# Six turns instead of three in a projection unit, and other addresses for the low halves, in a two-layer attention trunk on one core

## The chip, the core and the metric

One NeuronCore of a Trainium2 chip runs the whole program in one launch. The metric is device time in microseconds (us); lower is better. Three runs of the kernel before gave 625.53, 626.4 and 626.1, a median of 626.1 us.

## What is computed

A trunk of two layers over 256 tokens of 1024 channels, in float32. Each layer normalises its input, multiplies it by one wide matrix of 9808 columns, and cuts the result into the operands of three token mixers (a causal one, one that keeps 64 keys chosen by an indexer, and one with forget gates), their SiLU gates, and three sets of merge gates:

```python
h = rms_norm(x, gain)
proj = jnp.einsum('bsd,de->bse', h, w_in)
...
y = jnp.einsum('nbsw,nwd->bsnd', jnp.stack([oa, ob, oc], axis=0), w_branch)
gates = jax.nn.sigmoid(merge_logit).reshape(B, S, N_BRANCH, D_MODEL)
merged = jnp.sum(gates * y, axis=2)
return x + jnp.einsum('bsd,de->bse', merged, w_out)
```

A final RMS norm follows the second layer.

## The kernel before

Every large product is made of three products of rounded parts. An operand is split into a high half (the value rounded to the matmul's float32r type) and a low half (the rest), and high times high, high times low and low times high are summed in PSUM. So a weight tile `raw` becomes `wh` (ScalarE, line 364) and `wl` (VectorE, line 368), 128x1024 each, in rings of six buffers. The normalised, transposed input of a layer lies in `hTh` and `hTl`; gated mixer outputs lie in `og0h`, `og0l`, `og1h`, `og1l`; the merged result of a layer is put into the two buffers `V` that held the mixers' values.

TensorE's work comes in units, each of which fills one PSUM bank. `unit_b` (line 419) makes 128 projected columns for all 256 tokens: 16 matmuls with `wh` as stationary operand, going through `hTh` and `hTl` of each of eight blocks in turn, and 8 matmuls with `wl`, which meet `hTh` alone. All 24 move 256 columns and all load weights of their own. There are 130 such units. `unit_y` (line 867) multiplies gated outputs by the branch matrices: 12 matmuls of 256 columns, in 48 units. `unit_a` (line 435) has the weights as the moving operand, mostly 512 columns, and `hTh`/`hTl` (mixer values) or the merged halves (output projection) as the stationary one.

The order in a unit is a list `g`, cut into four operations for the planner (line 429):

```python
g = his[:8] + los[:2] + his[8:11] + los[2:5] + his[11:] + los[5:]
for a, b in ((0, 8), (8, 13), (13, 21), (21, 24)):
```

A step from a `wh` matmul to a `wl` matmul is called a turn here; a unit has three, after 8, 11 and 16 of the `wh` matmuls. The second comes behind a matmul that moves `hTh`, the others behind one that moves `hTl`.

Nothing of the order is left to the hardware's queues: `Plan.run` (line 137) goes through all operations with estimated durations and puts them on the engines, for each engine the ready operation of the lowest key among those that could start soonest. A unit's key is its number; the splits of its weights have that number less `SPLIT_LEAD` (line 41), and attention steps (scores, transposes of the probabilities on line 678, products with the values on lines 695 to 700) have keys of their own. Such steps go between a unit's four operations, never inside one. I call a stretch of such steps inside or between units a block.

A tile's address in SBUF follows from the order in which tiles are made. Bytes modulo 512 of the tiles that matter: `wh` 128, `wl` 0, `hTh` and `hTl` both 192, both `V` buffers 128, the `og` tiles 192.

Of the kernel before, what the change touches and what calls it, by code (L numbers as in the profile page):

```python
# [9 lines left out]
F32 = mybir.dt.float32  # L10
F32R = mybir.dt.float32r
# [4 lines left out]
S = 256  # L16
# [3 lines left out]
KC = D // 128  # L20
# [17 lines left out]
       ("DVE", "DVE"): 127.0, ("ACT", "ACT"): 127.0, ("POOL", "POOL"): 100.0, ("ACT", "SP"): 1500.0, ("DVE", "SP"): 1500.0}  # L38
SEM = 70.0
HALF = 95.0  # L40
SPLIT_LEAD = 2.0
MARGIN = 200.0
QK_MARGIN = 1000.0
WARM = 14
MTH = 8
NC1 = 4
DMA_KEY = (-95, -94, -85, -84)
HI_KEY = (-60, -48, -47, -46)
NB1 = 2
EARLY = 1.5  # L50
HT_KEY = (-50, -49.5, -46.8, -46.2)
BANKS = ("proj", "s", "t", "o")
# [176 lines left out]
def t_mm(n):  # L229
    return 1.3 + 0.4434 * n  # L230
# [3 lines left out]
def hybrid_trunk(ctx, tc, x, norm_gain, w_in, forget_bias, w_branch, w_out, final_gain, consts, out):  # L234
# [3 lines left out]
    pool = ctx.enter_context(tc.tile_pool(name="sb", bufs=1))  # L238
# [3 lines left out]
    plan = Plan()  # L242

    def tag(name, n, shape, dt=F32):
        plan.tag(name, [pool.tile(shape, dt, name=f"{name}{i}") for i in range(n)])
# [4 lines left out]
    def T(b):  # L250
        return b.slot[1]
# [7 lines left out]
    def act(fn, n, ps, reads, writes, key, name="", extra=0.0, touch=()):  # L259
        return plan.op([("ACT", t_act(n, ps) + extra, fn)], reads, writes, key, 0.0, name, touch)  # L260

    def dve(fn, n, reads, writes, key, name="", cost=None, touch=(), port=False):
        o = plan.op([("DVE", cost or t_dve(n), fn)], reads, writes, key, 0.0, name, touch)
        o.port = port
        return o
# [6 lines left out]

    wh = [pool.tile([128, 1024], F32R, name=f"wh{i}") for i in range(R_RING)]
    fz = pool.tile([128, 6, 16], F32, name="fz")
    wl = [pool.tile([128, 1024], F32R, name=f"wl{i}") for i in range(R_RING)]
    fbias = pool.tile([128, L, 8], F32, name="fbias")
    csum = pool.tile([128, 2, 8], F32, name="csum")
    V = [pool.tile([128, 2, 8, 128], F32R, name=f"v{i}") for i in range(2)]  # L280
    qs = [[pool.tile([128, S], F32R, name=f"q{p}{i}") for i in range(3)] for p in "hxy"]
    gT = pool.tile([128, L, KC], F32, name="gT")
    hTh = pool.tile([128, KC, S], F32R, name="hTh")
    hTl = pool.tile([128, KC, S], F32R, name="hTl")
    og = [[pool.tile([128, 4, S], F32R, name=f"og{i}{p}") for p in "hl"] for i in range(2)]
    NBD = 3
    bd = [[pool.tile([128, 2, S], F32R, name=f"bd{i}{p}") for p in "hl"] for i in range(NBD)]
# [15 lines left out]
    isc = pool.tile([128, 384], F32, name="isc")  # L303
    selb = pool.tile([128, 384], F32, name="selb")
    wf = pool.tile([128, S], F32, name="wf")
    cT = wf[:, :]
    half = pool.tile([128, 1], F32, name="half")
    small = pool.tile([128, 2, 4], F32, name="small")
    fsum = pool.tile([128, 2, 5], F32, name="fsum")
    ncs = pool.tile([128, 2, 8], F32, name="ncs")  # L310
    widx = pool.tile([128, 2, 8], F32, name="widx")

    k_id, k_rope, k_gT, k_bdz, k_cst, k_fb, k_wf, k_widx, k_lf, k_cs, k_main = (Tok() for _ in range(11))
    k_cT, k_row = Tok(), [Tok() for _ in range(6)]
# [7 lines left out]
    k_V = [[[Tok() for _ in range(2)] for _ in range(4)] for _ in range(2)]  # L322
    k_og = [[[Tok() for _ in range(4)] for _ in range(2)] for _ in range(2)]
    k_acc = [Tok() for _ in range(KC)]

    tag("raw", R_RAW, [128, 2048])
    plan.tag("wh", wh)
    plan.tag("wl", wl)
# [4 lines left out]
    plan.tag("ptl", pts[1:])  # L333
    plan.tag("bd", bd)
    for nm, n, cols, dt in (("rsh", 2, S, F32), ("rr", 2, S, F32),
                            ("th", 2, S, F32), ("g", 4, S, F32), ("e", 4, 384, F32), ("st", 8, 8, F32),
                            ("fb", 2, 384, F32), ("ot", 2, S, F32), ("t8", 4, 8, F32), ("mth", MTH, S, F32)):
        tag(nm, n, [128, cols], dt)
    ptag("proj", 3)
    ptag("s", 2)  # L340
# [6 lines left out]
    def piece(key, ckey, ap, cshape, sel, shape, k):  # L347
# [18 lines left out]
        def lo():  # L366
            p[1].v = T(p[1])[:, :a * b].rearrange("p (a b) -> p a b", a=a)
            DVE.tensor_tensor(p[1].v, sel(c.v), p[0].v.bitcast(F32), op=ALU.subtract)  # L368
        act(hi, a * b, False, [c], [p[0]], k - SPLIT_LEAD, f"hi {key}")
        dve(lo, a * b, [c, p[0]], [p[1]], k - SPLIT_LEAD, f"lo {key}", port=True)  # L370
        return p
# [31 lines left out]
    def mm_ops(o, terms, cost, writes, key, name, first, last, main=False):  # L403

        n = len(terms)

        def emit():
            for i, (a, b, _) in enumerate(terms):
                PE.matmul(o(), a(), b(), start=first and i == 0, stop=last and i == n - 1)  # L409
        reads = list({id(r): r for t in terms for r in t[2]}.values())  # L410
        pe(emit, cost * n, reads, writes + ([k_main] if main else []), key, name)
# [3 lines left out]
    def unit(name):  # L415
        units[0] += 1
        return units[0] - 1
# [3 lines left out]
    def unit_b(name, get, npart=128):  # L421
        u = unit(name)
        p = get(u)
        ps = Buf("proj")
        o = lambda: T(ps)[:npart, :S]
        his = [(lambda k=k: p[0].v[:, k], lambda k=k, h=h: h[:, k], [p[0]] + hT_all[i])
               for k in range(KC) for i, h in enumerate((hTh, hTl))]
        los = [(lambda k=k: p[1].v[:, k], lambda k=k: hTh[:, k], [p[1]] + hT_all[0]) for k in range(KC)]
        g = his[:8] + los[:2] + his[8:11] + los[2:5] + his[11:] + los[5:]
        for a, b in ((0, 8), (8, 13), (13, 21), (21, 24)):  # L430
            mm_ops(o, g[a:b], t_mm(256), [ps], u, name, a == 0, b == 24, True)
        return u, ps

# [16 lines left out]
    def rope(ps, key, np_=128):  # L450
        c, s = rope_t
        sh, r = Buf("rsh"), Buf("rr")
        a = lambda: T(ps)[:np_, :S]
        dve(lambda: DVE.stream_shuffle(T(sh)[:np_], a(), SWAP), S, [ps], [sh], key, "rope")  # L454
        gps(lambda: POOL.tensor_tensor(T(sh)[:np_], T(sh)[:np_], s[:np_], op=ALU.mult), S, [k_rope], [sh], key, "rope")  # L455
        dve(lambda: DVE.tensor_tensor(T(r)[:np_], a(), c[:np_], op=ALU.mult), S, [ps, k_rope], [r], key, "rope")  # L456
        gps(lambda: POOL.tensor_tensor(T(r)[:np_], T(r)[:np_], T(sh)[:np_], op=ALU.add), S, [sh], [r], key, "rope")  # L457
        return r

    def new_bd():  # L460
        b = Buf("bd")
        return b, [[Tok(), Tok(), Tok()] for _ in range(2)]
# [133 lines left out]
    class Pair:  # L596
# [3 lines left out]
        def ev_q(self, ps, key):  # L600
            key -= EARLY
            if self.mixer == "c":
                self.q = write_q((lambda: T(ps)[:, :S], ps), True, key, -0.125)
            else:
                r = rope(ps, key)
                self.q = write_q((lambda: T(r), r), False, key, -0.125)

        def ev_k(self, ps, key):
            self.k, self.kt = new_bd()
            src = ps if self.mixer == "c" else rope(ps, key - EARLY)  # L610
            write_bd(src, self.k, self.kt, key - EARLY, self.mixer == "c")
            self.attend(key + 1)

        def ev_g(self, ps, key):
            th = Buf("th")
            g = self.g = Buf("g")
            key -= EARLY
            act(lambda: ACT.activation(T(th), T(ps)[:, :S], AF.Tanh, scale=0.5), S, True, [ps], [th], key, "g")
# [22 lines left out]
        def attend(self, key):  # L641
# [43 lines left out]
            o = Buf("o")  # L685
            v = V[self.vi]

# [163 lines left out]
    def unit_m(l, n, j, gates):  # L851
        c0 = COL["mg"] + n * D + (j // 2) * 256
        u, ps = unit_b(f"m{n}{j}", lambda k: win_b(l, c0, j % 2, k))
        if n == 0:
            act(lambda: ACT.activation(acc[:, j], T(ps)[:, :S], AF.Tanh, scale=0.5), S, True, [ps], [k_acc[j]], u - EARLY, "mth")
            return
        th = gates[n, j] = Buf("mth")
        act(lambda: ACT.activation(T(th), T(ps)[:, :S], AF.Tanh, scale=0.5), S, True, [ps], [th], u - EARLY, "mth")

    def merged(j):  # L860
        v = V[j // 4].rearrange("p t h c -> p (t h c)")
        i = j % 4
        return [v[:, (2 * i + p) * S:(2 * i + p + 1) * S] for p in range(2)]

    k_mg = [k_V[j // 4][j % 4] for j in range(KC)]

    def unit_y(l, n, j, oi, gates, rank):
        u = unit(f"y{n}{j}")
# [73 lines left out]
    def v_units(l, m, vi):  # L942
        gets = [lambda k, i=i: rows_a("A", w_in, l, COL["v" + m], i, k) for i in range(4)]
        for t in range(2):
            ra = [lambda k, p=p, t=t: [k_hT[p][t][k]] for p in range(2)]
            u, ps = unit_a(f"v{m}{t}", gets, t, hA[0], hA[1], ra)
            v_out(ps, t, vi, [ps], u)

    def v_out(ps, t, vi, deps, key):
        hi, lo = V[vi][:, t, :, :64], V[vi][:, t, :, 64:]  # L950
        src = lambda: T(ps).rearrange("p (h c) -> p h c", h=8)
        kv = [k for i in (2 * t, 2 * t + 1) for k in k_V[vi][i]]
        act(lambda: ACT.activation(hi, src(), AF.Copy), W, True, deps, kv, key, "v", touch=[ps])
        dve(lambda: DVE.tensor_tensor(lo, src(), hi.bitcast(F32), op=ALU.subtract), W, deps, kv, key, "v", touch=[ps])
# [69 lines left out]
    def alternate(a, b):  # L1024
        r = []
        for i in range(0, max(len(a), len(b)), 2):
            r += a[i:i + 2] + b[i:i + 2]
        return r
# [4 lines left out]
    for l in range(L):  # L1033
# [21 lines left out]
        v_units(l, "b", 0)  # L1055
        for f in between(mixer(l, "b", 0, 0), alternate(y_of(l, 2, 1, 1, gates, range(8)), m_of(l, 1, gates, range(NB1)))):
            f()
        for f in m_of(l, 1, gates, range(NB1, 8)) + y_of(l, 1, 0, 2, gates, range(8)):
            f()
# [49 lines left out]
```

## Time and profile before

| | |
|---|---|
| median of three runs | 626.1 us (625.53 to 626.4) |
| the profiled execution | 625.54 us, span 623.6 us |
| PE busy | 612.1 us, 98% of the span, 4808 matmuls |
| DVE busy | 541.2 us, 87% |
| ACT busy | 450.6 us, 72% |
| POOL busy | 89.1 us, 14% |
| read from HBM | 103.37 MB |
| granted TensorE clock | 0.999 of full speed |

The profiled execution is 0.56 us under the median. A matmul's recorded duration (some 278 ns for 256 columns) is longer than the distance from one start to the next, since matmuls overlap; so the starts in the order of time, and not the durations, tell how fast PE goes.

### The profile page before, as it was taken

The numbers are of one execution on the slowest core, as the hardware profiler recorded it, in microseconds if no ns is written. First come the engines' busy times: TensorE is split into PE (matmuls) and PEld (weight loads), VectorE is DVE, ScalarE is ACT, GpSimd is POOL, SyncE is SP. The second block draws the span as 40 slices with busy tenths as digits, with TensorE's granted clock in tenths as the row PEclk, the third lists the DMA queues.
The fourth block names the chain that finished last, engine by engine and source line by source line (L and its number), as shares of the span: only waits on it lengthen the run. The fifth ranks groups of instructions, "written<-read, shape, count | busy, mean of one in ns | idle before, by whom it ended". The sixth has DMA issues, their size and how long they took to land.

```text
span 623.6 us, 12663 instructions
## 1 busy us (share of the span) xinstructions
PE 612.1 (98%) x4808; PEld 584.8 (94%) x4808; DVE 541.2 (87%) x1328; ACT 450.6 (72%) x943; POOL 89.1 (14%) x100
## 2 busy tenths in 40 slices
PE   8999999999999999999999999999999999999996
PEld 6999999999998999999889999998999989999975
DVE  8899999975998899979589999998589978999673
ACT  5788498776886679855587867995679756987541
POOL 1242131000000223200005303200000013122001
PEclk9999999999999999999999999999999999999999
DMA  9954534586463653375455545457635465343811
GB/s 300 292 182 157 167 120 150 165 280 201 138 204 102 209 166 121 115 240 200 157 181 164 197 152 171 146 168 243 209 101 189 146 206 173 128 136 115 292 34 68
DMA packets 96156, 107.32 MB, mean 172 GB/s; under 512 B 4576, under 2 KB 84832, under 8 KB 96096
## 3 DMA queue, kind: packets, MB, share of 16 engines
q1 hardware_dynamic: 95808, 106.13, 52.3%
q8 instruction: 37, 0.61, 0.4%
q10 hardware_dynamic: 288, 0.39, 0.2%
q14 instruction: 23, 0.19, 0.1%
HBM read 103.37 MB, written 1.05 MB: 167 GB/s over the span
## 4 chain that ended last, share of the span: by engine, by line
PE 63%; DVE 23%; ACT 8%; issue 3%; DMA 2%; POOL 0%; POOLq 0%; DVEq 0%
PE proj L409 56%; DVE wl L368 7%; ACT wh L364 3%; DVE isc L842 2%; PE s L590 2%; PE s L592 1%; PE t L678 1%; PE proj L988 1%; DVE t L841 1%; DMA raw<-in_w_out_dram 1%; DVE rsh L454 1%; ACT pth L681 1%; ACT e L655 1%; DVE ptl L683 1%; DVE e L651 1%
## 5 line engine op out<-in xcount | busy, mean ns | idle before, releaser
L368 DVE TENSOR_TENSOR wl<-raw,wh 128x1024 fp32r<-128x1024 f32 (+1 forms) x190 | 239.5, 1269 | 40.9 <-ACT wh L364 40.2
L409 PE MATMUL proj<-hTh,wh 128*128 128x256 f32 (+1 forms) x1040 | 258.7, 278 | 0.5 <-DVE qy L400 0.2
L409 PE MATMUL proj<-hTl,wh 128*128 128x256 f32 (+1 forms) x1040 | 257.2, 277 | 0.0
L364 ACT ACTIVATE wh<-raw 128x1024 fp32r<-128x1024 f32 (+1 forms) x190 | 199.1, 1056 | 69.3 <-PE proj L409 59.1
L409 PEld LDWEIGHTS proj<-hTh,wh 128*128 128x128 f32 (+1 forms) x1040 | 194.7, 187 | 2.1 <-DVE rr L456 0.5
L409 PEld LDWEIGHTS proj<-hTl,wh 128*128 128x128 f32 (+1 forms) x1040 | 194.7, 187 | 0.3
L409 PE MATMUL proj<-hTh,wl 128*128 128x256 f32 (+1 forms) x1040 | 186.1, 281 | 1.1 <-DVE wl L368 0.9
L409 PEld LDWEIGHTS proj<-hTh,wl 128*128 128x128 f32 (+1 forms) x1040 | 147.7, 187 | 1.8 <-DVE wl L368 1.7
L455 POOL TENSOR_TENSOR rsh<-rsh,cst 128x256 f32<-128x256 f32 (+1 forms) x42 | 32.2, 768 | 392.8 <-DVE rsh L454 391.9
L655 ACT ACTIVATE e<-e,st 128x128 f32<-128x128 f32 x96 | 42.6, 448 | 6.0 <-DVE st L651 5.7
L457 POOL TENSOR_TENSOR rr<-rr,rsh 128x256 f32<-128x256 f32 (+1 forms) x42 | 45.4, 1082 | 7.4 <-DVE rr L456 2.7
L409 PE MATMUL proj<-wh,v 128*128 128x512 f32 (+1 forms) x144 | 35.8, 369 | 0.5 <-DVE v L400 0.5
L409 PE MATMUL proj<-og0l,wh 128*128 128x256 f32 x128 | 33.8, 276 | 0.0
L409 PE MATMUL proj<-og0h,wh 128*128 128x256 f32 x128 | 32.5, 278 | 0.0
L409 PE MATMUL proj<-wh,hTh 128*128 128x512 f32 x80 | 31.8, 398 | 0.0
L409 PE MATMUL proj<-wh,hTl 128*128 128x512 f32 x80 | 31.3, 391 | 0.0
L409 PEld LDWEIGHTS proj<-wh,v 128*128 128x128 f32 x144 | 25.2, 188 | 5.6 <-DVE v L400 0.9
L409 PE MATMUL proj<-og0h,wl 128*128 128x256 f32 x128 | 28.6, 276 | 0.0
L683 DVE TENSOR_TENSOR ptl<-t,pth 128x384 fp32r<-128x384 f32 x48 | 25.8, 554 | 0.8 <-ACT pth L681 0.4
L715 ACT ACTIVATE ot<-o 64x256 f32<-64x256 f32 x48 | 18.3, 382 | 11.0 <-PE o L695 10.4
L409 PE MATMUL proj<-wl,hTh 128*128 128x512 f32 x80 | 24.9, 392 | 0.0
L409 PEld LDWEIGHTS proj<-og0h,wh 128*128 128x128 f32 x128 | 24.0, 188 | 0.0
(195 smaller groups left out, 1057.1 us busy)
## 6 DMA issues: line engine op xcount, KB each, us to landing
raw<-in_w_in_dram SPq DMA_DIRECT2D x74, 1024.0 KB, 5.1
raw<-in_w_branch_dram SPq DMA_DIRECT2D x24, 512.0 KB, 3.4
raw<-in_w_out_dram SPq DMA_DIRECT2D x8, 1024.0 KB, 6.5
tmp<-wf SPq DMA_DIRECT2D x16, 128.0 KB, 5.5
raw<-in_w_in_dram SPq DMA_DIRECT2D x3, 512.0 KB, 6.1
x<-in_x_dram SPq DMA_DIRECT2D x4, 256.0 KB, 4.1
raw<-in_w_in_dram SPq DMA_DIRECT2D x2, 320.0 KB, 5.3
out_dram<-tmp SPq DMA_DIRECT2D x2, 320.0 KB, 2.6
```

Source lines behind the costliest of these rows:

```text
L364: ACT.activation(p[0].v, sel(c.v), AF.Copy)
L368: DVE.tensor_tensor(p[1].v, sel(c.v), p[0].v.bitcast(F32), op=ALU.subtract)
L409: PE.matmul(o(), a(), b(), start=first and i == 0, stop=last and i == n - 1)
L454: dve(lambda: DVE.stream_shuffle(T(sh)[:np_], a(), SWAP), S, [ps], [sh], key, "rope")
L455: gps(lambda: POOL.tensor_tensor(T(sh)[:np_], T(sh)[:np_], s[:np_], op=ALU.mult), S, [k_rope], [sh], key, "rope")
L457: gps(lambda: POOL.tensor_tensor(T(r)[:np_], T(r)[:np_], T(sh)[:np_], op=ALU.add), S, [sh], [r], key, "rope")
L590: PE.matmul(o.rearrange("p (h c) -> p h c", h=2), qh[:, sl], kl[:, :, :n], start=True, stop=False)
L592: PE.matmul(o[:, h * n:(h + 1) * n], x[h][:, sl], kh[:, 0 if shared else h, :n], start=False, stop=h == 1)
L655: act(lambda t=t, a=a, n=n, e=e, st=st: ACT.activation(T(e)[:, a:a + n], T(e)[:, a:a + n], AF.Exp, bias=T(st)[:, t:t + 1], scale=-1.0, acc ...
L683: dve(lambda h=h, src=src: DVE.tensor_tensor(T(pl)[:, h], src(), T(ph)[:, h].bitcast(F32), op=ALU.subtract), 384, [ps, kp[h][0]], [kp[h][1 ...
L715: act(lambda r=r, h=h: ACT.activation(T(t)[r], T(o)[64:, h * S:(h + 1) * S], AF.Copy), S, True, [o], [kt[h]], key, "og", HALF, touch=[t])
L842: dve(lambda o=o, t8=t8: DVE.match_replace(o, T(t8), o, TAKEN), n, [t8], [k_isc[i]], key + r * step, "top8")
```

## The change

The 24 matmuls of a `unit_b` are put into another order with six turns, by a table of pairs (so many `wh`, then so many `wl`), and are cut into four operations of six. `SPLIT_LEAD` goes from 2.0 to 2.6. Small tiles move between others, so that `hTl` starts at 64 modulo 512 (`hTh` stays at 192), and one `V` buffer at 0 (the other stays at 128). The merged high halves now all lie in one `V` buffer and the low halves in the other, where before both halves of a block lay side by side in one buffer. Tiles of the table that aren't named keep their place modulo 512; `raw`, the work tiles behind it and the small `st` and `t8` tiles get other places. No instruction is added or taken away.

```diff
-SPLIT_LEAD = 2.0
+SPLIT_LEAD = 2.6
...
+UNIT_ORDER = ((6, 1), (3, 1), (3, 2), (2, 1), (1, 2), (1, 1))
...
     wl = [pool.tile([128, 1024], F32R, name=f"wl{i}") for i in range(R_RING)]
+    v1 = pool.tile([128, 2, 8, 128], F32R, name="v1")
     fbias = pool.tile([128, L, 8], F32, name="fbias")
     csum = pool.tile([128, 2, 8], F32, name="csum")
-    V = [pool.tile([128, 2, 8, 128], F32R, name=f"v{i}") for i in range(2)]
+    V = [pool.tile([128, 2, 8, 128], F32R, name="v0"), v1]
...
     hTh = pool.tile([128, KC, S], F32R, name="hTh")
+    half = pool.tile([128, 1], F32, name="half")
+    small = pool.tile([128, 2, 4], F32, name="small")
+    fsum = pool.tile([128, 2, 5], F32, name="fsum")
+    ncs = pool.tile([128, 2, 8], F32, name="ncs")
+    widx = pool.tile([128, 2, 8], F32, name="widx")
+    t8 = [pool.tile([128, 8], F32, name=f"t8{i}") for i in range(4)]
     hTl = pool.tile([128, KC, S], F32R, name="hTl")
+    st = [pool.tile([128, 8], F32, name=f"st{i}") for i in range(4)]
...
-        g = his[:8] + los[:2] + his[8:11] + los[2:5] + his[11:] + los[5:]
-        for a, b in ((0, 8), (8, 13), (13, 21), (21, 24)):
+        g, i, j = [], 0, 0
+        for nh, nl in UNIT_ORDER:
+            g += his[i:i + nh] + los[j:j + nl]
+            i, j = i + nh, j + nl
+        n = UNIT_ORDER[0][0]
+        for a, b in ((0, n), (n, 12), (12, 18), (18, 24)):
...
     def merged(j):
-        v = V[j // 4].rearrange("p t h c -> p (t h c)")
-        i = j % 4
-        return [v[:, (2 * i + p) * S:(2 * i + p + 1) * S] for p in range(2)]
+        return [v.rearrange("p t h c -> p (t h c)")[:, j * S:(j + 1) * S] for v in V]
-    k_mg = [k_V[j // 4][j % 4] for j in range(KC)]
+    k_mg = [[k_V[p][j // 2][j % 2] for p in range(2)] for j in range(KC)]
```

How the order moves is seen at three places. The first is PE, in the `unit_b` that fills bank 161 from weight buffers 64 and 71 in layer 0 (`proj` is the bank, then the activations and the weights); before, from its seventh matmul on:

```order
L409 MATMUL proj_161<-hTh,wh_64 128x256
L409 MATMUL proj_161<-hTl,wh_64 128x256
L409 MATMUL proj_161<-hTh,wl_71 128x256 x2
L409 MATMUL proj_161<-hTh,wh_64 128x256
L409 MATMUL proj_161<-hTl,wh_64 128x256
L409 MATMUL proj_161<-hTh,wh_64 128x256
L409 MATMUL proj_161<-hTh,wl_71 128x256 x3
```

and the same unit now, from its seventh matmul on:

```order
L417 MATMUL proj_161<-hTh,wl_71 128x256
L417 MATMUL proj_161<-hTh,wh_64 128x256
L417 MATMUL proj_161<-hTl,wh_64 128x256
L417 MATMUL proj_161<-hTh,wh_64 128x256
L417 MATMUL proj_161<-hTh,wl_71 128x256
L417 MATMUL proj_161<-hTl,wh_64 128x256
L417 MATMUL proj_161<-hTh,wh_64 128x256
L417 MATMUL proj_161<-hTl,wh_64 128x256
L417 MATMUL proj_161<-hTh,wl_71 128x256 x2
```

The first turn has come two matmuls earlier, and two of the six turns now come behind `hTh` instead of one of three.

The second place is PE again, where a pair of heads of the forget mixer in layer 0 has its probabilities transposed (`t` is a PSUM bank, `e` the probabilities); before:

```order
L409 MATMUL proj_159<-hTl,wh_68 128x256
L678 MATMUL t_165<-cst,e_131 128x128 x3
L678 MATMUL t_164<-cst,e_132 128x128 x3
L409 MATMUL proj_159<-hTh,wl_75 128x256 x3
L409 MATMUL proj_160<-hTh,wh_63 128x256
```

and now:

```order
L417 MATMUL proj_161<-hTl,wh_63 128x256
L690 MATMUL t_164<-cst,e_144 128x128 x3
L417 MATMUL proj_161<-hTh,wh_63 128x256
L417 MATMUL proj_161<-hTl,wh_63 128x256
L417 MATMUL proj_161<-hTh,wl_70 128x256 x2
L417 MATMUL proj_161<-hTh,wh_63 128x256
L417 MATMUL proj_161<-hTl,wh_63 128x256
L690 MATMUL t_165<-cst,e_145 128x128 x3
L417 MATMUL proj_161<-hTh,wl_70 128x256
```

Transposes of two heads stood together and now have six matmuls of a unit between them. Over the whole program, blocks that stand before a `unit_b` or `unit_y` matmul go from 83 to 100.

The third place is DVE while the indexer of layer 0 chooses its keys (`isc` are the scores, lines 842 and 854 the step that strikes out the eight largest); before:

```order
L842 MATCH_REPLACE isc<-t_149,isc 128x128
L842 MATCH_REPLACE isc<-t_150,isc 128x256
L368 TENSOR_TENSOR wl_72<-raw_119,wh_65 128x1024
L841 MAX t_147<-isc 128x8
L841 MAX t_148<-isc 128x8
L842 MATCH_REPLACE isc<-t_147,isc 128x128
L842 MATCH_REPLACE isc<-t_148,isc 128x256
L368 TENSOR_TENSOR wl_73<-raw_120,wh_66 128x1024
L368 TENSOR_TENSOR wl_74<-raw_120,wh_67 128x1024
```

and now:

```order
L376 TENSOR_TENSOR wl_72<-raw_131,wh_65 128x1024
L376 TENSOR_TENSOR wl_73<-raw_132,wh_66 128x1024
L853 MAX t_96<-isc 128x8
L853 MAX t_97<-isc 128x8
L854 MATCH_REPLACE isc<-t_96,isc 128x128
L854 MATCH_REPLACE isc<-t_97,isc 128x256
L376 TENSOR_TENSOR wl_74<-raw_132,wh_67 128x1024
```

One split has moved ahead of one round of the choice; the next stays where it was.

## Rows read from the trace of the kernel before

**Rows 1.** The page's busy times, shares of the span and instructions:
```profile
PE 612.1 (98%) x4808; PEld 584.8 (94%) x4808; DVE 541.2 (87%) x1328; ACT 450.6 (72%) x943; POOL 89.1 (14%) x100
```

**Rows 2.** Busy time by stretch: us, then PE, PEld, DVE, ACT, POOL, clock, DMA:
```profile
58.00:104.00 46.00, 44.94 (x385) 44.06 (x385) 44.43 (x145) 34.43 (x79) 10.67 (x12) 1.00 0.45 142
134.00:291.00 157.00, 156.83 (x1319) 153.61 (x1318) 135.29 (x332) 116.39 (x248) 17.47 (x18) 1.00 0.52 169
```

**Rows 3.** PE in order of time (start us, us), an uninterrupted unit and the next one's start:
```profile
137.30 0.28 PE L409 MATMUL proj<-hTh,wh 128*128 128x256 f32 x1
...
140.02 0.28 PE L409 MATMUL proj<-hTh,wh 128*128 128x256 f32 x1
```

**Rows 4.** The same view, a unit behind a block:
```profile
172.03 0.28 PE L409 MATMUL proj<-hTh,wh 128*128 128x256 f32 x1
...
172.86 0.28 PE L409 MATMUL proj<-hTl,wh 128*128 128x256 f32 x1
172.98 0.40 PE L409 MATMUL proj<-hTh,wl 128*128 128x256 f32 x2
...
173.45 0.28 PE L409 MATMUL proj<-hTh,wh 128*128 128x256 f32 x1
173.56 0.50 PE L409 MATMUL proj<-hTh,wl 128*128 128x256 f32 x3
...
174.81 0.28 PE L409 MATMUL proj<-hTh,wh 128*128 128x256 f32 x1
```

**Rows 5.** The same view, two heads' transposes together, then the rest of a unit:
```profile
165.86 0.84 PE L678 MATMUL t<-cst,e 128*128 128x128 f32 x6
166.46 0.48 PE L409 MATMUL proj<-hTh,wl 128*128 128x256 f32 x2
166.78 0.28 PE L409 MATMUL proj<-hTh,wh 128*128 128x256 f32 x1
...
168.44 0.28 PE L409 MATMUL proj<-hTh,wh 128*128 128x256 f32 x1
```

**Rows 6.** The same view, the first unit, whose weights have 80 columns:
```profile
21.84 0.28 PE L409 MATMUL proj<-hTh,wh 128*80 128x256 f32 x1
...
22.66 0.28 PE L409 MATMUL proj<-hTl,wh 128*80 128x256 f32 x1
22.77 0.40 PE L409 MATMUL proj<-hTh,wl 128*80 128x256 f32 x2
...
24.65 0.28 PE L409 MATMUL proj<-hTh,wh 128*128 128x256 f32 x1
```

**Rows 7.** The same view, a turn late in layer 1:
```profile
573.10 0.28 PE L409 MATMUL proj<-hTl,wh 128*128 128x256 f32 x1
573.22 0.39 PE L409 MATMUL proj<-hTh,wl 128*128 128x256 f32 x2
```

**Rows 8.** The same view, 24 matmuls of 512 columns: output projection, then mixer values:
```profile
296.64 1.08 PE L409 MATMUL proj<-wh,v 128*128 128x512 f32 x4
...
302.19 0.39 PE L409 MATMUL proj<-wh,v 128*128 128x512 f32 x1
...
502.12 0.39 PE L409 MATMUL proj<-wh,hTh 128*128 128x512 f32 x1
...
507.63 0.28 PE L409 MATMUL proj<-hTh,wh 128*128 128x256 f32 x1
```

**Rows 9.** The same view, one head's transposes alone:
```profile
91.36 0.51 PE L678 MATMUL t<-cst,e 128*128 128x128 f32 x3
91.63 0.60 PE L409 MATMUL proj<-hTh,wl 128*128 128x256 f32 x3
```

**Rows 10.** The same view, two turns at which PE stood:
```profile
88.35 0.28 PE L409 MATMUL proj<-hTl,wh 128*128 128x256 f32 x1
89.06 0.39 PE L409 MATMUL proj<-hTh,wl 128*128 128x256 f32 x1 [0.43 <-DVE wl L368]
...
103.77 0.50 PE L409 MATMUL proj<-hTh,wl 128*128 128x256 f32 x2 [0.50 <-DVE wl L368]
```

More of the change, by code (lines that the diff above doesn't have):

```diff
@@ L305, in hybrid_trunk @@
     wf = pool.tile([128, S], F32, name="wf")
+    st += [pool.tile([128, 8], F32, name=f"st{i}") for i in range(4, 8)]
     cT = wf[:, :]
[L307 to L311, printed above, removed]
     k_id, k_rope, k_gT, k_bdz, k_cst, k_fb, k_wf, k_widx, k_lf, k_cs, k_main = (Tok() for _ in range(11))
@@ L324, in hybrid_trunk @@
     k_acc = [Tok() for _ in range(KC)]
+    plan.tag("st", st)
+    plan.tag("t8", t8)
     tag("raw", R_RAW, [128, 2048])
@@ L335, in hybrid_trunk @@
     for nm, n, cols, dt in (("rsh", 2, S, F32), ("rr", 2, S, F32),
-                            ("th", 2, S, F32), ("g", 4, S, F32), ("e", 4, 384, F32), ("st", 8, 8, F32),
-                            ("fb", 2, 384, F32), ("ot", 2, S, F32), ("t8", 4, 8, F32), ("mth", MTH, S, F32)):
+                            ("th", 2, S, F32), ("g", 4, S, F32), ("e", 4, 384, F32),
+                            ("fb", 2, 384, F32), ("ot", 2, S, F32), ("mth", MTH, S, F32)):
         tag(nm, n, [128, cols], dt)
```

## The prediction

> **What bounds the kernel now.** I read the busy times first: PE is busy for 612.1 us of 623.6 [rows 1], so what counts is how fast PE's matmuls follow each other. The busy time by stretch then says where another engine is as full. In 58 to 104 us, where layer 0 chooses its keys, DVE is busy for 44.43 of 46 us and PE for 44.94; in the 157 us of branch products and two mixers PE has 156.83 and DVE 135.29 [rows 2]. So PE alone sets the time nearly everywhere, and in that one stage a faster PE would only stand and wait for DVE. The clock is granted in full in both (1.00, the 2.4 GHz level), so no step below is one of the clock.
>
> Then PE in the order of time. An undisturbed unit of 24 matmuls lasts from 137.30 to 140.02, 2.72 us or 113.3 ns each [rows 3]. Behind a block it is another picture: from 172.03 to 173.45 twelve matmuls take 1.42 us, 118.3 each, and from 173.56 to 174.81 eleven take 1.25 us, 113.6 each [rows 4]. The same operands, the same shapes, no wait: there is a slow cadence, some 4.8 ns a matmul longer, that begins when PE comes back from a block and ends all at once. It ended here at the second turn, not at the first (172.86 to 172.98). In the unit behind two heads' transposes it went on through two turns: fourteen matmuls from 166.78 to 168.44 take 118.6 each [rows 5].
>
> I took the start of each matmul of 256 columns that moves `hTh`, `hTl` or an `og` tile, and the next one's start. Of 3,696 such steps 999 are 2 to 20 ns over 113.3, in sum 4.83 us; the first starts at 21.84 [rows 6], the last at 573.10 [rows 7]. 104 of them with 0.50 us lie in the stage of 58 to 104 us. What ends the slow cadence: of 43 turns behind a matmul that moves `hTh` and is slow 31 ended it, of 54 turns behind `hTl` 8 did (the first of these 97, at 22.66, didn't [rows 6], the last, at 573.10, did [rows 7]); steps from `hTh` to `hTl` under `wh` seldom. At a turn the address of the weights that are loaded moves by 128 bytes modulo 512; in between, from one `wh` matmul to the next, nothing moves modulo 512.
>
> **The change, part by part.** *Six turns.* A unit's turns behind `hTh` go from one to two, those behind `hTl` from two to four, and they come earlier. With an end in 0.72 and 0.15 of them (31 of 43, 8 of 54 rounded) I walked along PE's order of both programs, slow from each block on: 1,133 slow matmuls before (999 measured, so the rates are about right) and 755 now. The ratio 0.67 takes from the 895 slow matmuls outside the DVE stage (4.33 us) 4.33 x 0.33 = 1.4 us. That already counts that the blocks go from 83 to 100.
>
> *128 bytes between `hTh` and `hTl`.* No row shows such a step of the moving operand in these units, so it has bounds. At best it does at each matmul what a turn does, and the slow cadence is gone: 4.33 us in all, 2.9 more than the turns alone. At worst no unit settles any more. The first unit is the nearest row for that: its weights have 80 columns, so their address moves by 320 bytes a block, and its 24 matmuls take 2.81 us, 117.1 each, without ever settling [rows 6]. I take half of the gain that is left, 1.45 us, because the row nearest in kind, the turn, is itself a step of 128 bytes: it ends the slow cadence in 39 of 97 cases and never began it in an undisturbed unit [rows 3].
>
> So the trace has two cadences of equal work, 113.3 and 118.3 ns [rows 4]. It doesn't show that addresses are the cause. A rule speaks against this part: by the Trainium skill, "TensorE: Matmul & The Clock Gate", Part 2, step 1, the array has two separate read ports, and loading the next weights takes no read bandwidth from the running matmul; addresses would then change nothing, this term would be 0 and the sum 1.45 us higher. The two cadences are something that this rule has no place for.
>
> *Merged halves and 512 columns.* Where weights move, a matmul takes 5.55 us / 24 = 231.3 ns in the output projection and 5.51 / 24 = 229.6 in the mixer values [rows 8], against 2 x 113.3 = 226.7. 168 and 240 of them lose 0.8 + 0.7 = 1.5 us. The new addresses can take that away or double it; I take 0, and keep -1.5 and +1.5.
>
> *More blocks.* Two heads' transposes together take 0.60 us up to the next unit's matmul, and the two matmuls behind 0.48 instead of the 0.39 that two take elsewhere [rows 5]; one head's take 0.27, with 0.60 for three matmuls instead of 0.51 [rows 9]. Two alone cost 2 x (0.27 + 0.09) = 0.72 against 0.69, 0.03 us more. For 17 blocks: +0.5 us.
>
> *Splits and waits.* Two of PE's waits for `wl`, 0.43 and 0.50 us, are in the DVE stage [rows 10]. The first `wl` is now wanted two matmuls, 0.23 us, earlier, and of the splits there one moves ahead of a round of the choice and the next stays. DVE's work is the same, so what PE gains there it waits again: I take 0 for the stage, with bounds of -1.4 (the two waits and 0.5 us of slow cadence go) and +0.5 (two waits 0.23 longer). Elsewhere the splits are ahead; a lead of 2.6 units instead of 2.0 costs nothing as long as DVE keeps 14% of its time free, as in 134 to 291 us [rows 2]. No DMA, no instruction and no queue is added; SP's issues keep their number, POOL's work is the same 89.1 us [rows 1].
>
> **Sum:** 625.54 - 1.4 - 1.45 + 0.5 = 623.2 us for an execution like the profiled one. That one is 0.56 under the median of 626.1; against the median the same 2.4 us give 623.7.
>
> **Rivals.** *A: the step of 128 bytes ends the slow cadence at once.* 4.33 us go, and half of the 1.5 us in the 512-column units: 626.1 - 4.3 - 0.7 + 0.5 = 621.6. For it: the slow cadence ends only where an address moves. Against it: the first unit, where addresses move and nothing settles.
>
> *B: nothing comes of it.* If loading weights doesn't disturb the running matmul, and turns ended the cadence only because time had passed (one behind `hTl` did in 8 of 54 cases), the slow stretches stay as long, and blocks and earlier `wl` add 0.5 and up to 0.5: 626.6, from 625.5 to 627.1. That is what the page of the Trainium skill named above would make of it. This is also the case that the change doesn't do what it says.
>
> *C, the other side: the alternation keeps units from settling.* The place is the `wh` part of each `unit_b`, the mechanism that the distance between the address that moves and the one that is loaded changes at each matmul, as in the first unit [rows 6]. If the 1,040 matmuls that move `hTl` all take the 4.84 ns, of which some 29% do now (909 of 3,120 in `unit_b` are slow), that is 740 x 4.84 = 3.6 us: 626.1 + 3.6 + 0.5 = 630.2; with all matmuls of `unit_b` slow 2,211 x 4.84 = 10.7 and 637. It decides from the point at which more matmuls are slow than 999.
>
> **How the numbers follow.** The forecast has 0.36, A 0.26, B 0.20, C 0.18. The forecast's own range is 622.3 to 625.4. The range of all runs from 620.0 (A with most of the 512-column gain) to 628.0 (B with a little more, or a weak C); C from 629 on is left out. A measurement tells 0.2% from no change, that is 624.85 and 627.35. Faster: 0.34 of the forecast's 0.36 and all of A, 0.60. Same: most of B and the forecast's rest, 0.20. Slower: C and B's upper end, 0.20.
>
> **What would show it.** In the changed profile a unit behind a block should go back to 113.3 ns within some four to six matmuls instead of about twelve; undisturbed units must still take 2.72 us. Blocks of transposes should more often stand alone. PE's wait for `wl` around 58 to 104 us should be about as long as now or longer. The forecast is wrong if undisturbed units take more than 2.75 us (C), if the slow cadence behind a block lasts as long as before (B), or if PE waits for `wl`, probabilities or scores elsewhere by more than 2 us.

## The result and the profile after

The changed kernel takes 632.21 us in the median (631.92 to 633.15, four runs), the kernel before beside it 625.82 us (624.76 to 626.4): a ratio of 1.0107, 95% interval 1.0089 to 1.0125. It is slower, by five times what a measurement can tell here, and outside the range. The profiled execution took 632.34 us with a span of 630.4; before it was 625.54 and 623.6.

The page's busy times, which answer to [rows 1]:

```profile
PE 619.6 (98%) x4808; PEld 594.4 (94%) x4808; DVE 535.9 (85%) x1318; ACT 456.6 (72%) x953; POOL 91.4 (15%) x100
```

Busy time by stretch, the same columns as [rows 2]:

```profile
58.00:104.00 46.00, 44.26 (x376) 43.54 (x375) 43.17 (x147) 34.10 (x77) 10.72 (x12) 1.00 0.42 134
134.00:291.00 157.00, 156.96 (x1300) 154.35 (x1300) 131.15 (x318) 118.22 (x252) 17.64 (x18) 1.00 0.51 167
```

PE does the same 4808 matmuls and is busy 7.5 us longer. In 134 to 291 us it has no more room than before and gets 1300 matmuls done instead of 1319, with the clock granted in full. The planner gave ten scalings of probabilities to ACT that were DVE's, so DVE lost work and ACT gained some; neither sets the end. In the page's chain of work PE alone now holds 89% of the span; before it held 63%, and DVE 23%.

PE in the order of time (start us, us), an undisturbed unit that answers to [rows 3]:

```profile
147.85 0.28 PE L417 MATMUL proj<-hTh,wh 128*128 128x256 f32 x1
147.97 0.28 PE L417 MATMUL proj<-hTl,wh 128*128 128x256 f32 x1
...
148.55 0.28 PE L417 MATMUL proj<-hTh,wl 128*128 128x256 f32 x1
148.67 0.29 PE L417 MATMUL proj<-hTh,wh 128*128 128x256 f32 x1
...
150.68 0.28 PE L417 MATMUL proj<-hTh,wh 128*128 128x256 f32 x1
```

147.85 to 150.68 is 2.83 us, 117.9 ns a matmul, where [rows 3] have 2.72. The turn at 148.55 ends nothing. So it is in every unit: of the 78 units that ran uninterrupted before, 52 took 2.72 us; of 81 now none does, and their median is 2.829. A unit on `og` tiles, whose addresses agree modulo 512 as before, followed by a unit on `hTh` and `hTl`, shows where the slow cadence begins, in the same view:

```profile
158.53 0.28 PE L417 MATMUL proj<-og0h,wh 128*128 128x256 f32 x1
...
159.66 0.39 PE L417 MATMUL proj<-og0h,wl 128*128 128x256 f32 x2
159.89 0.28 PE L417 MATMUL proj<-hTh,wh 128*128 128x256 f32 x1
160.00 0.28 PE L417 MATMUL proj<-hTl,wh 128*128 128x256 f32 x1
160.12 0.28 PE L417 MATMUL proj<-hTh,wh 128*128 128x256 f32 x1
...
161.19 0.28 PE L417 MATMUL proj<-hTl,wh 128*128 128x256 f32 x1
161.30 0.28 PE L602 MATMUL s<-bd0l,qh 128*128 128x256 f32 x1
```

Twelve `og` matmuls from 158.53 to 159.89 take 1.36 us (113.3 each), the twelve behind them to 161.30 take 1.41 (117.5). No block stands between them: the step between `hTh` and `hTl` itself breaks a settled run. All eight places of this kind in the profiled execution give 117.5 ns for the twelve matmuls behind; in e1 below, where `hTl` is back at its place, all eight stay at 113.3.

I cut PE's time from its first matmul to its last into the steps at 113.3 ns per 256 columns and what is over that, in one execution of each kernel (a step is the time from one matmul's start to the next one's):

| us over, in the profiled execution | before | after |
|---|---|---|
| units on `hTh`, `hTl`, `og`: up to 20 ns over | 4.91 | 14.41 |
| other matmuls: up to 20 ns over | 2.01 | 2.02 |
| 20 to 119 ns over (entry into blocks, and in them) | 20.93 | 19.58 |
| over 119 ns (waits) | 10.71 | 9.38 |
| first to last matmul | 616.06 | 622.89 |

The slow cadence costs 9.50 us more, and 1.35 + 1.33 come back from blocks and waits; with +0.01 that is the 6.83 us between the two. Slow matmuls, counted as the prediction did, go from 999 to 2,781 of 3,696. The wait for `wl` in the stage in which keys are chosen is one long one now, where [rows 10] have 0.43 and 0.50:

```profile
86.32 0.44 PE L690 MATMUL t<-cst,e 128*128 128x128 f32 x2 [0.66 <-ACT e L675]
87.84 0.39 PE L417 MATMUL proj<-hTh,wl 128*128 128x256 f32 x1 [1.08 <-DVE wl L376]
```

### The profile page after: what moved, and what is told of

Its sections match the earlier page's. It is cut to its first block, busy times and chain, and to the rows that moved or that the text cites. A ratio compares the mean times of both kernels' runs of the same rounds, so it can differ in the third digit from the quotient of the medians.

```text
span 630.4 us, 12652 instructions
## 1 busy us (share of the span) xinstructions
PE 619.6 (98%) x4808; PEld 594.4 (94%) x4808; DVE 535.9 (85%) x1318; ACT 456.6 (72%) x953; POOL 91.4 (15%) x100
## 4 chain that ended last, share of the span: by engine, by line
PE 89%; DVE 5%; ACT 3%; issue 1%; DMA 1%; SPq 0%; POOL 0%; POOLq 0%; ACTq 0%; DVEq 0%
PE proj L417 78%; PE t L690 2%; PE s L602 2%; PE s L604 2%; PE proj L998 1%; ACT wh L372 1%; DMA x<-in_x_dram 1%; DVE wl L376 1%; PE o L708 1%; PE o L712 1%; DVE isc L854 1%; DVE t L853 1%; ACT qx L589 1%; PE o L711 0%; PE o L707 0%
## 5 line engine op out<-in xcount | busy, mean ns | idle before, releaser
L417 PE MATMUL proj<-hTh,wh 128*128 128x256 f32 (+1 forms) x1040 | 276.6, 283 | 0.1
L417 PE MATMUL proj<-hTl,wh 128*128 128x256 f32 (+1 forms) x1040 | 274.7, 280 | 0.0
L417 PE MATMUL proj<-hTh,wl 128*128 128x256 f32 (+1 forms) x1040 | 239.1, 282 | 1.1 <-DVE wl L376 1.1
L417 PEld LDWEIGHTS proj<-hTh,wl 128*128 128x128 f32 (+1 forms) x1040 | 176.9, 188 | 1.3 <-DVE wl L376 1.3
L467 POOL TENSOR_TENSOR rsh<-rsh,cst 128x256 f32<-128x256 f32 (+1 forms) x42 | 33.5, 798 | 385.1 <-DVE rsh L466 385.1
L469 POOL TENSOR_TENSOR rr<-rr,rsh 128x256 f32<-128x256 f32 (+1 forms) x42 | 50.2, 1199 | 12.3 <-DVE rr L468 7.6
L690 PE MATMUL t<-cst,e 128*128 128x128 f32 x144 | 23.7, 274 | 0.7 <-ACT e L675 0.7
```

Of the source, the lines that this page charges most:

```text
L690: PE.transpose(T(ps)[:, i * 128:(i + 1) * 128], T(es[h])[:, i * 128:(i + 1) * 128], ident)
```

## The experiments

Theory: the step of 128 bytes between `hTh` and `hTl` keeps units from settling (rival C), and the other parts do little. Its rivals: the six turns or the earlier splits cost the time; or 64 modulo 512 is a bad place for `hTl`, whatever `hTh` has. "Slow" are the steps of the prediction, of 3,696, in the one profiled execution; "whole units" the uninterrupted `unit_b` of that execution, counted where they take 2.72 us to within 2 ns; the ratio is to the kernel before beside them (medians 625.42 to 625.72).

| kernel | us | ratio, 95% interval | slow | whole units at 2.72 us (median) |
|---|---|---|---|---|
| e1, the change but `hTl` as far as before | 624.97 | 0.9988 [0.9974, 1.0001] | 720 | 61 of 81 (2.720) |
| e2, only `hTl` 128 off | 630.86 | 1.0077 [1.0059, 1.0094] | 2,856 | 0 of 78 (2.833) |
| e3, only six turns | 625.67 | 0.9997 [0.9985, 1.001] | 658 | 64 of 82 |
| e4, only the lead of 2.6 | 625.77 | 0.9999 [0.9987, 1.0012] | 1,023 | 51 of 78 |
| e5, `hTh` and `hTl` both at 64 | 625.56 | 1.0001 [0.9991, 1.0012] | 952 | 58 of 78 |
| e6, `hTl` 256 off | 625.6 | 1.0002 [0.9993, 1.001] | 1,095 | 52 of 78 |
| e9, `hTl` 64 off | 630.97 | 1.0088 [1.0074, 1.0103] | 2,670 | 0 of 78 (2.827) |
| e7, `wl` at the place of `wh` | 631.69 | 1.0095 [1.008, 1.011] | 3,527 | 1 of 78 (2.827) |
| e10, `wl` 256 off `wh` | 631.44 | 1.0098 [1.0085, 1.0111] | 3,314 | 5 of 78 (2.827) |
| e11, `wl` 64 off `wh` | 630.4 | 1.0082 [1.0069, 1.0095] | 2,548 | 0 of 78 (2.830) |
| e8, six turns, lead 2.6, margin 500 | 625.64 | 0.9998 [0.9982, 1.0014] | 624 | 62 of 78 |
| e12, e1 with a cheaper estimate | 628.21 | 1.0043 [1.0029, 1.0057] | 704 | 56 of 81 |
| e13, turns all behind `hTh` | 625.18 | 0.9988 [0.9978, 0.9997] | 1,006 | 53 of 78 |
| e14, e1 with turns all behind `hTh` | 625.56 | 1.0002 [0.9989, 1.0015] | 691 | 61 of 81 |

### One part undone, one part alone

**e1**: the change, with `hTl` made right behind `hTh`.

```diff
     hTh = pool.tile([128, KC, S], F32R, name="hTh")
+    hTl = pool.tile([128, KC, S], F32R, name="hTl")
     half = pool.tile([128, 1], F32, name="half")
...
-    hTl = pool.tile([128, KC, S], F32R, name="hTl")
```

> The changed kernel with one tile moved: hTl made directly behind hTh, so both lie at 192 modulo 512 again; the small tiles follow behind it, and every other tile, the six turns, the lead of 2.6 and the merged halves stay as in the change. Theory 1 (the 128 bytes between hTh and hTl keep each unit from settling): undisturbed units return from some 2.82 us to 2.72, and the time falls by 7 to 10 us against the change, to 622.5 to 625. Theory 2 (the six turns, or the moved order, keep units from settling): units stay at 2.82 and the time at 631 to 633. Theory 3 (the merged halves or the lead cost the time): 631 to 633 with units of 2.72 only here and there.

One tile's place brings 632.21 down to 624.97. A unit in the order of time, 2.72 us:

```profile
46.27 0.28 PE L417 MATMUL proj<-hTh,wh 128*128 128x256 f32 x1
...
48.99 0.28 PE L417 MATMUL proj<-hTh,wh 128*128 128x256 f32 x1
```

**e2**: the kernel before, with small tiles made between `hTh` and `hTl`, as in the change.

```diff
     hTh = pool.tile([128, KC, S], F32R, name="hTh")
+    half = pool.tile([128, 1], F32, name="half")
+    small = pool.tile([128, 2, 4], F32, name="small")
+    fsum = pool.tile([128, 2, 5], F32, name="fsum")
+    ncs = pool.tile([128, 2, 8], F32, name="ncs")
+    widx = pool.tile([128, 2, 8], F32, name="widx")
+    t8 = [pool.tile([128, 8], F32, name=f"t8{i}") for i in range(4)]
     hTl = pool.tile([128, KC, S], F32R, name="hTl")
+    st = [pool.tile([128, 8], F32, name=f"st{i}") for i in range(4)]
...
```

> The kernel before with the small tiles moved so that hTl lies at 64 modulo 512 and hTh at 192; three turns, the lead of 2.0 and the mixed V buffers as before. Theory 1: slow throughout, 632 to 636 (no unit settles). Theory 2: as before, 625 to 627. Theory 3: 625 to 627.

The order is that of before, and the slow cadence is that of the change: 2.83 us a unit.

```profile
46.37 0.28 PE L414 MATMUL proj<-hTh,wh 128*128 128x256 f32 x1
...
49.20 0.28 PE L414 MATMUL proj<-hTh,wh 128*128 128x256 f32 x1
```

Together e1 and e2 settle which part of the change costs the time.

**e3** takes over the table `UNIT_ORDER` and the cuts of six, **e4** the one line `SPLIT_LEAD = 2.6`.

> The kernel before with the six turns and the cuts of six alone; addresses and the lead of 2.0 as before. Theory 1: units settle and do so earlier behind a block; 1 to 2 us faster than before, 623.8 to 625.2. Theory 2: units don't settle, 631 to 633. If turns shorten nothing and the extra blocks cost, 626 to 627.

> The kernel before with a lead of 2.6 units for the splits alone. Theories 1 and 2: 625 to 627, no change. Theory 3, with the lead at fault: 629 to 633.

e4 does nothing. e3 does what was forecast for the slow matmuls, 999 to 658, and yet it is no faster. In its profiled execution the time came back as waits. In the cut used above, from the first `unit_b` on (what lies ahead of it the six turns don't touch), 1.78 us of slow cadence, 0.43 of other matmuls and 0.37 of block costs went, and waits grew by 2.61, from 5.44 to 8.05: to the last matmul it is 595.28 us before and 595.30 in e3. PE's waits in e3 from 23 us on (engine, line, what it waited for: us in all, times, longest), mostly for DVE:

```profile
PE s L595 <- DVE st L656: 1.2, 2, 0.9
PE proj L410 <- DVE wl L369: 1.1, 2, 1.0
PE proj L410 <- DVE mth L894: 0.6, 2, 0.3
PE proj L410 <- DVE bd0l L744: 0.5, 1, 0.5
PE proj L410 <- DVE bd2l L744: 0.5, 1, 0.5
PE proj L410 <- DVE g L624: 0.5, 1, 0.5
```

and the same view of the kernel before, which waits less and for other things:

```profile
PE proj L409 <- DVE wl L368: 0.9, 2, 0.5
PE proj L409 <- DVE v L400: 0.5, 1, 0.5
PE proj L409 <- DVE qy L400: 0.2, 1, 0.2
PE proj L409 <- DVE bd0l L739: 0.2, 1, 0.2
```

Two of them in e3, in the order of time:

```profile
86.22 0.39 PE L410 MATMUL proj<-hTh,wl 128*128 128x256 f32 x1 [0.95 <-DVE wl L369]
...
410.24 0.38 PE L595 MATMUL s<-bd2l,qh 128*128 128x256 f32 x1 [0.88 <-DVE st L656]
```

### Distance or place

In **e5**, **e6** and **e9** the order is that of before and the same small tiles move: all ahead of `hTh` (`hTh` and `hTl` at 64), or some of them between the two (`hTl` at 448, then at 256, `hTh` at 192). The edit of e9:

```diff
     hTh = pool.tile([128, KC, S], F32R, name="hTh")
+    half = pool.tile([128, 1], F32, name="half")
+    small = pool.tile([128, 2, 4], F32, name="small")
     hTl = pool.tile([128, KC, S], F32R, name="hTl")
+    fsum = pool.tile([128, 2, 5], F32, name="fsum")
...
```

In e6 `fsum`, `ncs` and `widx` stand between them too.

> Three turns and lead 2.0 as before; the small tiles are moved ahead of hTh, so hTh and hTl both lie at 64 modulo 512. Every other address is as in the run with hTl alone at 64. Theory 1a (units don't settle because the place of the moving operand alternates): both at one place, so units settle as before, 624.5 to 627. Theory 1b (64 itself is a bad place against weights at 128 and 0): no unit settles, 631 to 640, more than with hTl alone since every matmul now moves from there.

> As the run with hTl at 64, but with the small tiles parted so that hTl lies at 448, 256 off hTh at 192. Theory 1a (any alternation hinders settling): units stay at some 2.83 us, 630 to 633. Rival 1c (128 is bad, 256 harmless, as a step that comes back to the same place every second time): units settle, 624.5 to 627.

> Three turns and lead as before; the small tiles are parted so that hTl lies at 256 modulo 512, 64 off hTh at 192. What is known: 128 off costs some 5 us, 0 off and 256 off nothing. If only the part of the step modulo 256 counts and any such part hinders settling: no whole unit at 2.72 us, 629 to 633. If 128 is the one bad step: units settle, 624.5 to 627.

A unit of e5:

```profile
45.98 0.28 PE L414 MATMUL proj<-hTh,wh 128*128 128x256 f32 x1
...
48.70 0.28 PE L414 MATMUL proj<-hTh,wh 128*128 128x256 f32 x1
```

of e6:

```profile
46.72 0.28 PE L414 MATMUL proj<-hTh,wh 128*128 128x256 f32 x1
...
49.44 0.28 PE L414 MATMUL proj<-hTh,wh 128*128 128x256 f32 x1
```

and of e9:

```profile
47.40 0.28 PE L414 MATMUL proj<-hTh,wh 128*128 128x256 f32 x1
...
50.23 0.28 PE L414 MATMUL proj<-hTh,wh 128*128 128x256 f32 x1
```

2.72, 2.72 and 2.83 us. The place 64 is harmless in itself, so it is the distance that counts. At 0 and 256 bytes modulo 512 units settle, at 64 and 128 none does. (Only 64 was tried as a place of both tiles.) In e5 the slow matmuls were shared out otherwise, 499 instead of 909 in units on `hTh` and `hTl`, 453 instead of 90 in those on `og`; I did not follow that up.

### The address of the loaded weights

**e7** makes `fz` behind `wl` instead of ahead of it, so that `wl` lies at 128 like `wh` and a turn moves no address modulo 512. **e10** and **e11** put small tiles between them: `wl` at 384 and at 192. The edit of e7:

```diff
     wh = [pool.tile([128, 1024], F32R, name=f"wh{i}") for i in range(R_RING)]
-    fz = pool.tile([128, 6, 16], F32, name="fz")
     wl = [pool.tile([128, 1024], F32R, name=f"wl{i}") for i in range(R_RING)]
+    fz = pool.tile([128, 6, 16], F32, name="fz")
```

> The kernel before with fz made behind wl instead of between wh and wl, so wl lies at 128 modulo 512 like wh, and no turn moves the address of the loaded weights modulo 512. If the step of 128 bytes at a turn is what ends the slow cadence: it hardly ends any more, slow matmuls rise from some 1,000 of 3,696 to 2,500 or more, 630 to 635. If a turn ends it in another way (the same activations twice running, or time): some 1,000 slow matmuls, 624.5 to 627.

> The kernel before with wl at 384 modulo 512, 256 off wh at 128, instead of 128 off. If a step of 256 is as good as none (as it was for the activations): turns don't end the slow cadence, as with wl at wh's place, some 3,500 slow matmuls of 3,696, 630 to 633. If any step of the weights ends it: some 1,000 slow, 624.5 to 627.

> The kernel before with wl at 192 modulo 512, 64 off wh at 128. If a turn's step works by any part modulo 256: the slow cadence ends at turns as before or sooner, 600 to 1,100 slow matmuls, 624 to 627. If it has to be 128: some 3,500 slow, 630 to 633.

A unit of e7, with a turn in it (47.63), takes 2.83 us from 46.68 to 49.51:

```profile
46.68 0.28 PE L409 MATMUL proj<-hTh,wh 128*128 128x256 f32 x1
...
47.63 0.40 PE L409 MATMUL proj<-hTh,wl 128*128 128x256 f32 x2
47.86 0.28 PE L409 MATMUL proj<-hTh,wh 128*128 128x256 f32 x1
...
49.51 0.28 PE L409 MATMUL proj<-hTh,wh 128*128 128x256 f32 x1
```

Of the turns behind slow matmuls none of 318 ended the slow cadence in e7 and none of 282 in e10; before it was 39 of 97. So with `wl` 0 or 256 bytes off no turn ends it. The one whole unit of e7 and the five of e10 that take 2.72 us had come out of a block already settled (three of e10's follow each other). A unit of e10, 2.82 us:

```profile
46.57 0.28 PE L411 MATMUL proj<-hTh,wh 128*128 128x256 f32 x1
...
49.39 0.28 PE L411 MATMUL proj<-hTh,wh 128*128 128x256 f32 x1
```

At 64 (e11) no whole unit takes 2.72 us, but the picture is another one: 33 of 78 take 2.77 us, and in these the `wh` matmuls take 113.4 ns in the mean and only the `wl` matmuls are slow, 120.0. One of them, with eight `wh` matmuls in 0.91 us and three `wl` matmuls in 0.36:

```profile
138.37 0.28 PE L411 MATMUL proj<-hTh,wh 128*128 128x256 f32 x1
...
139.28 0.40 PE L411 MATMUL proj<-hTh,wl 128*128 128x256 f32 x2
...
140.78 0.52 PE L411 MATMUL proj<-hTh,wl 128*128 128x256 f32 x3
141.14 0.28 PE L411 MATMUL proj<-hTh,wh 128*128 128x256 f32 x1
```

In e11 `wl` lies at 192, where `hTh` and `hTl` lie. The three runs move `wl` alone, and so its distance from `wh` and its place against the moving tiles change together; a run that moves `wh` and `wl` by the same bytes, as e5 does for the moving tiles, is missing. For the weights, then, 128 is the good one of the four values tried with `wh` at 128 and the moving tiles at 192, and whether as a distance or as a place isn't shown. For the moving tiles 128 is a bad distance.

### Why the six turns bring no time

**e8** is e3 with the lead of 2.6 and the planner's `MARGIN` at 500 instead of 200. **e12** is e1 with the planner's estimate of a matmul lowered, `0.5 + 0.4434 * n` instead of `1.3 + 0.4434 * n`. **e13** keeps the order and the plan of before and swaps `hTh` and `hTl` in two of a unit's eight blocks, so that all three turns come behind `hTh`; **e14** does the same for the six turns of e1.

```diff
+        his[6:8], his[14:] = his[7:5:-1], his[15:13:-1]
         g = his[:8] + los[:2] + his[8:11] + los[2:5] + his[11:] + los[5:]
```

> Addresses as before, six turns, lead 2.6, and a planner's margin of 500 ns instead of 200 before matmuls that wait for attention steps. If the 1.5 to 1.8 us that six turns took from the slow cadence came back as PE's waits for scores' operands and probabilities, a later place for those steps keeps some of them: 623 to 624.7. If the waits come from DVE's and ACT's own work: as with six turns alone, 625 to 626.

> The changed kernel with hTl back at hTh's place modulo 512, and the planner's price of a matmul 0.8 ns lower (114.0 instead of 114.8 ns for 256 columns), nearer to the mean of 114.2 that matmuls have once they settle sooner. If PE's waits for scores' operands and transposes come from a plan that thinks PE slower than it is: waits fall by 1 us or more, 623 to 624.5. If they come from the other engines' work: 624.5 to 625.8.

> The kernel before with the pairs of blocks 3 and 7 turned round (hTl before hTh) in each unit, so that all three turns come behind a matmul that moves hTh. Waits, operations, plan and the order of everything else stay as they are. If turns behind hTh end the slow cadence by their kind (31 of 43 against 8 of 54): slow matmuls fall from 1,000 to some 600 to 750 and 1.2 to 1.8 us of it go; the time falls by 0.5 to 1.8 us, to 623.7 to 625, as far as PE's waits for other engines don't take it back. If the kind doesn't matter, only where in the unit the turn stands: 1,000 slow, 625 to 626.

> The changed kernel with hTl back at hTh's place modulo 512 and the wh matmuls ordered so that each of the six turns comes behind hTh. Its plan is that of the run with hTl back. If the kind of turn matters: slow matmuls fall from 720 to 450 or fewer, 1 us or more less slow cadence. If what a plan of another engine's work takes back decides: waits of PE rise by as much and the time stays at 624.5 to 625.5; else 623.5 to 624.3.

e8 leaves 624 slow matmuls and the time as it was. e12 makes it worse, 628.21 us, with as few slow matmuls as e1: in its profiled execution waits from the first `unit_b` on take 8.88 us against 6.91 in e1, which is all of the 1.93 us between the two there. e13 should have told whether fewer slow matmuls without another plan bring time, but they did not get fewer: 40 of 97 turns ended the slow cadence, 39 of 97 before. Counted by place in the unit (with two or three turns more), the first turn ends it in 8 of 41 cases before and 10 of 42 in e13, the second in 31 of 45 and 30 of 44, the third in 0 of 13 and 1 of 14. The first and third come behind `hTl` before and behind `hTh` in e13: the place in the unit decides, and not the tile that was moved last. So e13 can't tell, and whether the waits grow because PE comes too early for DVE's results or because the plan puts the blocks elsewhere stays open. e13's 0.12% is under the 0.2% that can be told, though its interval just leaves out 1, and no row of its profile accounts for it. No version beats the kernel before clearly. The merged halves were not run alone.

## Why the prediction was wrong

**What bounds the kernel, and the two cadences: right.** PE sets the time, the cadences are 113.3 and some 118 ns, and they are what the change acts on. The quantity to watch was the number of slow matmuls: it rose from 999, as rival C had it. The sign of being wrong that the prediction had named, undisturbed units of more than 2.75 us, came with 2.83.

**The step that failed is "128 bytes between `hTh` and `hTl`".** The prediction took half of the best case, a gain of 1.45 us, "because the row nearest in kind, the turn, is itself a step of 128 bytes". The size of the step was the same and the operand was not. At a turn the loaded address moves, at each `hTh`/`hTl` pair the moving one. The runs show that the two don't want the same: 128 for the weights, of the values tried (e7, e10, e11), and 0 or 256 for the moving tiles (e2, e5, e6, e9). In place of -1.45 us the step alone cost +5.3 us (e2: 630.86 against 625.57), and within the whole change 7.2 (632.21 against e1's 624.97, which was measured at another time). That it "never began" a slow stretch in [rows 3] spoke only of turns. The nearest row in effect was the one that stood for the worst case, [rows 6]: a unit in which it never settles.

By the rule of the Trainium skill, "TensorE: Matmul & The Clock Gate", Part 2, step 1, this term would be 0 if, as the prediction did, one takes it to say that addresses change nothing, since loading weights takes no read bandwidth from the running matmul. The runs don't agree with 0: moving nothing but addresses costs 0.8 to 1.0% (e2, e7, e9, e10, e11). What makes it so was not measured.

**Rival C was right in the place and the price, and its mechanism was too wide.** It gave 630.2 to 637 us; 632.21 came. 1,782 more matmuls are slow, 1,605 of them in `unit_b`, between its 740 and 2,211. Its mechanism was that the distance between the moving and the loaded address changes at each matmul. It does so in e6 too, by 256 bytes, and there units settle. Left out of C was that other costs would shrink: of 9.50 us of slow cadence, 2.7 were given back in blocks and waits.

**Six turns: the count right by luck, the time wrong.** Forecast was a factor of 0.67 on slow matmuls; measured 658 / 999 = 0.66 (e3) and 720 / 999 = 0.72 (e1). But 1.4 us did not come out of it: e3's ratio is 0.9997. "Splits and waits", taken as 0, was the place: waits from the first `unit_b` on grew by 2.61 us in e3 and 1.47 in e1, in one execution each. The bound of +0.5 that the prediction gave waits looked at the stage of 58 to 104 us. There they stayed as they were (1.55 us before, 1.51 in e3), and from 104 to 410 us they grew by 2.98. The chances behind the count, 0.72 for a turn behind `hTh` and 0.15 behind `hTl`, were no property of the kind of turn: with all turns behind `hTh` as many end it as before (e13), and in e3 itself 16 of 36 behind `hTh` end it (0.44) and 40 of 75 behind `hTl` (0.53). So the factor of 0.67 came out with other chances than those that it was made of.

**More blocks: +0.5 not seen.** With 99 blocks the costs in that class fell by 0.37 us in e3 from the first `unit_b` on. **The lead: 0, and 0 measured** (e4). **512 columns: 0 forecast**; the excess of such matmuls (steps up to 20 ns over) is 1.61 us before, 1.78 after, 1.82 in e1 and 1.60 in e3, so the new places of the merged halves cost at most some 0.2.

**The wait for `wl` in 58 to 104 us** was to be as long as now or longer: 1.08 against 0.43 + 0.50, right.

## What to carry to other kernels

Where matmuls with loads of their own follow each other, look at the starts of equal matmuls in a row: two cadences of equal work say that addresses may count, and then each pair of tiles that alternates wants its own distance, to be measured by moving small tiles, before it is put into a larger change. A rule found for the operand that is loaded isn't one for the operand that moves. And time taken off the bounding engine in many small pieces can come back as waits for a second engine, so count the waits of the new plan and not only the pieces.

## What was unexpected of the hardware

With 256 columns in float32r and weights loaded for each matmul, the distance of two alternating moving tiles modulo 512 bytes decides between 2.72 us (0 or 256) and 2.83 us (64 or 128) for 24 matmuls, at the same granted clock (0.997 to 0.999). For the loaded weights, of the distances tried between the two kinds only 128 gives 2.72; with 0 or 256 bytes the same unit takes 2.83, and with 64 it takes 2.77 or some 2.83. The cadence has a memory: in e7 one whole unit of 78, and in e10 five, did run at 2.72 us though no turn there ends a slow run. So a run that comes settled out of a block can stay settled, and what a turn with `wl` 128 off does is to end a slow one. In the change the opposite step, of the moving address, broke a settled run at its first pair (159.89).
